# Two edits at the attention's joint: the norm weights' loads are queued behind the output units' loads, and the second tokens' queries are computed in two halves of the features

## The chip, the cores and the metric

One core of a Trainium2 chip runs the whole kernel. The metric is device time in microseconds (us). Three runs of the kernel before gave a median of 1199.4 us (1196.8 to 1199.63). One more execution was taken with the hardware profiler: it took 1191.01 us, with a span of 1189.2 us from the first to the last recorded instruction. All durations below come from that one execution.

## The reference, cut to what matters

The network has two layers of width 1024 over 256 tokens. Around the change each layer does this (l is the layer, `ng` its eight norm weights):

```
h = mixer(...)                                  # layer 0: RWKV and retention, layer 1: sparse attention and short convolution
x = x + rms_norm(concat(y_a, y_b) @ w_out, ng[3])
q = (rms_norm(x, ng[4]) @ wq)                   # 256 tokens x 512 features, 4 heads of 128
s = q . k * 128**-0.5 ; prob = softmax(s)       # k and v of 256 memory tokens, computed earlier
x = x + rms_norm((prob . v) @ wo, ng[5])
x = x + 0.5 * rms_norm(swiglu(rms_norm(x, ng[6])), ng[7])
```

So at the joint of mixer and attention two norms follow each other: weight `ng[3]` on the mixer's output, and, after the sum into x, weight `ng[4]` ahead of the query projection.

## The kernel before

The 256 tokens are two tiles of 128 tokens, called t = 0 and t = 1. Every weight is taken in units of 128 x 1024 numbers. A unit is loaded by a DMA of SyncE's queue (SP) into a staging tile `wst`, rounded by ScalarE (ACT) into a high part `whi` ("hi"), and VectorE (DVE) subtracts that from the unit to get the low part `wlo` ("lo"). A product is then three matmuls (high by high, low by high, high by low) that add up in one PSUM bank. A PSUM bank holds 512 float32 numbers in each of 128 partitions, and one call of `bank` takes one whole bank.

`cross` is the function of the change, and it runs once in each layer. It first takes four output units of the mixer (`w_out`, the "head"), each with its load, hi and lo. The other four output units (the "tail") open a list `units_ahead`, followed by the four units of `wq`, the four of `wo` and those of the next FFN. `ahead.load(n)` issues the next n loads; later each `lo` issues one load more. Of every five loads of the list the first three go to a ring of three staging tiles, the fourth and fifth to a ring of two in the pool "norm". The norm weights (`gain`, tile `gb`, 128 x 1024, one row copied to all partitions, ring of three in that same pool) are loaded on SP's queue too, and the call of `tc.issue_after` puts each behind the load that was written last before it. For the rest, what is not fixed in this way on SP stands in the order of the framework's planner.

From `bridge` on, the order of TensorE (PE), DVE and ACT is the order in which the code is written (`in_order`). The part that the second edit touches runs as follows for each layer. PE turns the last normalized tokens (`trh`), and projects the first half of the sums for the queries of t = 1 (`project` with the wq units 0 and 1: 12 matmuls of 512 columns into the bank `pq[1]`). Then it computes the scores of t = 0 (`scores`, tile `psc`), and with units 2 and 3 the second half of the sums for the queries of t = 1 (12 more matmuls into the same bank). Meanwhile DVE works on the lo's, finds each row's maximum (`highest`), and ACT takes the exponentials of t = 0 (`exps`, four instructions and their sums). Behind those stands `query(1)` on ACT, a copy of the bank (tile `qn`), on which PE's transposes `trq` (`query_t(1)`) wait.

In `project`, matmuls for unit j are written as 4 matmuls with the high part of the tokens (line 429), and 2 with the low part, one unit later (line 434). The retention code of layer 0 has four small products into one bank, each copied out by ACT before the next one is written (lines 1271 and 1272). They are not changed, but the prediction reads them.

Of the kernel before, what the change touches and what calls it, by code (L numbers as in the profile page):

```python
# [10 lines left out]
F32 = mybir.dt.float32  # L11
F32R = mybir.dt.float32r
AF = mybir.ActivationFunctionType
# [4 lines left out]
P = 128  # L18
# [76 lines left out]
def tile_hybrid_trunk(ctx: ExitStack, tc: tile.TileContext, a: dict, out: bass.AP, stop=None):  # L95
    nc = tc.nc
# [12 lines left out]
    def bank(tag, name):  # L109
        return psum.tile([P, 512], F32, name=name, tag=tag)  # L110
# [7 lines left out]
    def new_h(p, shift=48):  # L118

        return tuple(p.tile([P, DT * S + 64], F32R, name=name, bufs=1)[:, shift:shift + DT * S].rearrange(  # L120
            "p (k n) -> p k n", k=DT) for name in ("hhi", "hlo"))
# [80 lines left out]
    def wload(w, k0, kt, c0, n):  # L202
        src = w[k0 * P:(k0 + kt) * P, c0:c0 + n].rearrange("(k p) n -> p k n", p=P)
        def load(t):
            env["loaded"] = nc.sync.dma_start(t, src).ins

        return [load], kt, n
# [4 lines left out]
    def nat(w, n=512):  # L212
        return [wload(w, 2 * i, 2, 0, n) for i in range(4)]

    class units_ahead:
# [22 lines left out]
        def hi(self):  # L238
            st, kt, n, *only = self.staged.pop(0)
            hi, lo, v = unit_tiles(kt, n, *only)  # L240
            nc.scalar.activation(hi[:, :kt * n], st[:, :kt * n], AF.Copy)  # L241
            self.open.append((st, hi, lo, kt * n))
            self.units.append((v(hi), v(lo)))

        def lo(self):
            st, hi, lo, m = self.open.pop(0)
            env["split"] = nc.vector.tensor_sub(lo[:, :m], st[:, :m], f32(hi[:, :m])).ins  # L247
            self.load()
# [57 lines left out]
    def gain(ap, offset):  # L306
        g = env["norm"].tile([P, D], F32, name="gb", bufs=3)
        if "loaded" in env:
            with behind(env["loaded"]):
                row(g, ap, offset, D, eng=nc.sync)  # L310
        else:
            row(g, ap, offset, D)
        return g
# [99 lines left out]
    ng = lambda l, i: gain(a["norm_g"], (l * 8 + i) * D)  # L413
# [4 lines left out]
    def in_order():  # L418
        return tc.manual_schedule(engines={ET.DVE, ET.Activation, ET.PE})

    def project(ps, h, t, us, js):

        s = slice(t * P, (t + 1) * P)
        for j in (*js, None):
            if j is not None:
                for i in range(2):
                    k = 2 * j + i
                    for n in range(2):
                        nc.tensor.matmul(ps, h[0][:, k, s], us[j][n][:, i, :], start=k == 0 and n == 0, stop=False)  # L429
            if j != js[0]:  # L430
                p = js[-1] if j is None else js[js.index(j) - 1]
                for i in range(2):
                    k = 2 * p + i
                    nc.tensor.matmul(ps, h[1][:, k, s], us[p][0][:, i, :], start=False, stop=k == DT - 1)
# [188 lines left out]
    def cross(l, sp, y, w_unit, w_out, kts):  # L623
# [4 lines left out]
        h, h2 = new_h(sp), new_h(sp)  # L628
        cx = ExitStack()
        xp = cx.enter_context(tc.tile_pool(reuse_waits="tile", name=f"xa{l}", bufs=1))  # L630
        gp, gn = ng(l, 3), ng(l, 4)
        head = len(kts) - 4

        def products(pss, t, q, y, us, first, last, ks, js):
            s, c = slice(t * P, (t + 1) * P), slice(q * 512, (q + 1) * 512)
            for j in js:
                k, u = ks[j], us[j]
                mm3(pss[t][q], (y[0][:, k, s], y[1][:, k, s]), (u[0][:, 0, c], u[1][:, 0, c]), first and j == 0,
                    last and j == len(ks) - 1)

        pss = [[bank(tag, "po") for tag in ("iv", "bk")] for _ in range(2)]
        for i in range(head):
            u = w_unit(kts[i])
            for t in range(2):
                for q in range(2):
                    products(pss, t, q, y, [u], i == 0, False, [kts[i]], (0,))
        tail = kts[head:]
        ahead = units_ahead([(*wload(w_out, k, 1, 0, D), wpool) for k in tail] + nat(wq) +
                            [wload(wo, k, 1, 0, D) for k in range(4)] + nat(wg) + nat(wu), env["norm"])
        ahead.load(5)  # L650
        kT = xp.tile([P, 4, S], F32, name="kT")
        vM = xp.tile([P, 2, 512], F32, name="vM")
        wsrc["i"] = 0
# [11 lines left out]
        o = new_h(keep, 0)  # L665
        pq, qn, qT, pr, mx, sm, pT, sps, nb = [{} for _ in range(9)]

        def query(t):
            qn[t] = xp.tile([P, 512], F32, name="qn", bufs=2)
            nc.scalar.activation(qn[t], pq[t], AF.Copy)  # L670

        def query_t(t):
            tr = bank("pa", "trq")
# [53 lines left out]
        def warm():  # L727
            nc.scalar.activation(small.tile([P, 1], F32, name="warm", tag="rstd"), ones, AF.Exp)

        with in_order():  # L730
            V = nc.vector
            hi, lo, units = ahead.hi, ahead.lo, ahead.units
            po = [post(pss[t], gp, t, False) for t in range(2)]
            no = [rms(env["x"][:, t, :], gn, h, t) for t in range(2)]
            tp = lambda t, q: products(pss, t, q, y, us, head == 0, True, tail, range(4))
            bridge(tp, po, no, ahead, 2 + l * 0)
            pq[0] = bank("pa", "pq")
            project(pq[0], h, 0, units, (0, 1, 2))
            po[1].root()
            po[1].gain(1)  # L740
            gn2 = ng(l, 6)
            warm()
            hi()
            po[1].add(0)
            po[1].add(1)
            no[1].square(0)
            no[1].gain(0)
            no[1].square(1)
            no[1].root()
            no[1].gain(1)  # L750
            project(pq[0], h, 0, units, (3,))
            query(0)
            no[1].scale(0, V)
            no[1].scale(1)
            no[1].turn(0)
            query_t(0)
            no[1].turn(1)
            lo()
            hi()
            lo()  # L760
            pq[1] = bank("pa", "pq")
            project(pq[1], h, 1, units, (0, 1))
            hi()
            lo()
            scores(0, 0)
            highest(0, 0)
            scores(0, 1)
            highest(0, 1)
            exps(0, 0)
            exps(0, 1)  # L770
            project(pq[1], h, 1, units, (2, 3))
            soft(0)
            query(1)
            hi()
            lo()
            query_t(1)
            soft_t(0)
            scores(1, 0)
            highest(1, 0)
            hi()  # L780
            lo()
            exps(1, 0)
            values(0)
            scores(1, 1)
            highest(1, 1)
            exps(1, 1)
            hi()

            pss = [[bank(tag, "po") for tag in ("iv", "bk")] for _ in range(2)]
            tp = lambda t, q, js=range(4): products(pss, t, q, o, units[4:8], True, True, range(4), js)  # L790
            po = [post(pss[t], gp2, t, False) for t in range(2)]
            no = [rms(env["x"][:, t, :], gn2, h2, t) for t in range(2)]
            tp(0, 0)
            soft(1)
            lo()
            hi()
            po[0].square(0)
            po[0].gain(0)
            lo()
            tp(0, 1, (0, 1))  # L800
            soft_t(1)
            hi()
            lo()
            tp(0, 1, (2, 3))
            po[0].square(1)
            po[0].root()
            values(1, 0, 2)
            po[0].gain(1)
            values(1, 2, 4)
            po[0].add(0)  # L810
            po[0].add(1)
            no[0].square(0)
            no[0].gain(0)
            no[0].square(1)
            no[0].root()
            no[0].gain(1)
            hi()
            tp(1, 0)
            no[0].scale(0, V)
            no[0].scale(1)  # L820
            lo()
            tp(1, 1, (0, 1, 2))
            no[0].turn(0)
            no[0].turn(1)
            po[1].square(0)
            po[1].gain(0)
            tp(1, 1, (3,))
            po[1].square(1)
            po[1].root()
            po[1].gain(1)  # L830
            hi()
            lo()
            pg = bank("pa", "pg")
            project(pg, h2, 0, units[8:12], range(4))
            po[1].add(0)
            po[1].add(1)
            hi()
            no[1].square(0)
            no[1].gain(0)
            no[1].square(1)  # L840
            no[1].root()
            no[1].gain(1)
            lo()
            no[1].scale(0, V)
            no[1].scale(1)
            hi()
            lo()
            pu = bank("pa", "pu")
            project(pu, h2, 0, units[12:16], (0, 1))
            no[1].turn(0)  # L850
            no[1].turn(1)
            project(pu, h2, 0, units[12:16], (2, 3))
# [767 lines left out]
    with stage("0", None, None, 4) as sp:  # L1620
        env["x"] = sp.tile([P, 2, D], F32, name="x", bufs=1)
        h = new_h(sp)
# [70 lines left out]
```

## Time and profile before

| what | value |
|---|---|
| median of 3 runs | 1199.4 us (1196.8 to 1199.63) |
| the profiled execution, span | 1191.01 us, 1189.2 us |
| PE busy, of the span | 96% |
| DVE busy | 61% |
| ACT busy | 51% |
| DMA, mean | 180 GB/s |
| granted PE clock, mean | 0.994 |

Busy shares are means over stages with different limits. PE's 96% says that almost any stall of PE adds to the span, and that few such stalls are left. `cross` fills about 404 to 485 us in layer 0 and 933 to 1008 us in layer 1, and shows several of them. In a timeline each row has its start, its length, the engine, the line, output <- inputs, the tile and the count; in square brackets stands how long the engine was idle before it, and what it waited for. PEld is PE's loading of the stationary operand, which runs beside the matmuls. The rows of matmuls overlap, so that their pace is read from their starts.

### The profile page before, as it was taken

To read this page: it belongs to the slowest core of one execution; us is meant where nothing else is said; L and a number is where in the kernel's file an instruction comes from. 1 tells how busy PE (TensorE), PEld (TensorE's weight loads), DVE (VectorE), ACT (ScalarE), POOL (GpSimd) and SP (SyncE) were. 2 spreads that over 40 slices of the span, in tenths; PEclk is the share of its full clock that TensorE was granted. 3 is DMA by queue.
4 is the path that set the end of the run, shared out by engine and by line. 5 is a ranking of instruction groups with operands and counts; after the bars stand their busy time and mean duration, and the time that the engine had idled before them with its cause. 6 is when DMAs were issued, how large, how long until landed. Compare 5 with 4: busy or idle time off the path is not lost.

```text
span 1189.2 us, 19763 instructions
## 1 busy us (share of the span) xinstructions
PE 1144.7 (96%) x7956; PEld 1011.5 (85%) x7956; DVE 728.5 (61%) x1097; ACT 606.8 (51%) x908; POOL 69.2 (6%) x104
## 2 busy tenths in 40 slices
PE   6999999999998999999999999999999999999997
PEld 4899999987776777899999799999788778899996
DVE  5546656587666678655554756544679577655552
ACT  5545555754334467554443645443556566554441
POOL 0000000011341000000000000000100000000000
PEclk9999999999999999999999999999999999999999
DMA  6777764644552765477665377665423753676650
GB/s 218 229 265 230 219 208 159 204 138 126 156 158 89 212 247 163 134 238 214 192 190 165 108 252 226 197 198 150 141 89 93 254 204 106 214 226 198 194 161 36
DMA packets 152267, 213.99 MB, mean 180 GB/s; under 512 B 21872, under 2 KB 115184, under 8 KB 152176
## 3 DMA queue, kind: packets, MB, share of 16 engines
q1 hardware_dynamic: 138224, 206.58, 56.0%
q10 hardware_dynamic: 13216, 3.54, 1.3%
q0 software_dynamic: 736, 2.62, 0.6%
q8 instruction: 62, 1.02, 0.3%
q14 instruction: 29, 0.24, 0.1%
HBM read 206.67 MB, written 6.05 MB: 179 GB/s over the span
## 4 chain that ended last, share of the span: by engine, by line
PE 78%; DVE 10%; ACT 4%; DMA 3%; issue 3%; POOL 2%; SPq 0%; ACTq 0%; POOLq 0%; DVEq 0%
PE pd L257 6%; PE pd L256 6%; PE pd L258 6%; PE pg L256 6%; PE pu L256 6%; PE pg L257 6%; PE pg L258 6%; PE pu L258 6%; PE pu L257 6%; PE pu L429 1%; PE trh L353 1%; DVE wlo L247 1%; DVE wlo L199 1%; PE pg L429 1%; POOL rstd L304 1%
## 5 line engine op out<-in xcount | busy, mean ns | idle before, releaser
L199 DVE TENSOR_TENSOR wlo<-wst,whi 128x1024 fp32r<-128x1024 f32 x290 | 355.2, 1229 | 291.3 <-ACT whi L198 289.8
L198 ACT ACTIVATE whi<-wst 128x1024 fp32r<-128x1024 f32 x290 | 306.0, 1060 | 314.8 <-PE pg L257 57.9
L256 PE MATMUL pu<-hhi,whi 128*128 128x256 f32 x576 | 160.8, 279 | 0.0
L256 PE MATMUL pg<-hhi,whi 128*128 128x256 f32 x576 | 160.7, 279 | 0.0
L258 PE MATMUL pu<-hhi,wlo 128*128 128x256 f32 x576 | 160.5, 279 | 0.0
L257 PE MATMUL pu<-hlo,whi 128*128 128x256 f32 x576 | 160.5, 279 | 0.0
L257 PE MATMUL pg<-hlo,whi 128*128 128x256 f32 x576 | 160.5, 279 | 0.0
L258 PE MATMUL pg<-hhi,wlo 128*128 128x256 f32 x576 | 160.4, 279 | 0.0
L257 PE MATMUL pd<-wlo,ahi 128*128 128x512 f32 x352 | 138.1, 393 | 0.0
L256 PE MATMUL pd<-whi,ahi 128*128 128x512 f32 x352 | 137.7, 392 | 0.0
L258 PE MATMUL pd<-whi,alo 128*128 128x512 f32 x352 | 137.7, 392 | 0.0
L256 PEld LDWEIGHTS pg<-hhi,whi 128*128 128x128 f32 x576 | 108.2, 188 | 1.4
L257 PEld LDWEIGHTS pg<-hlo,whi 128*128 128x128 f32 x576 | 108.2, 188 | 1.4
L258 PEld LDWEIGHTS pu<-hhi,wlo 128*128 128x128 f32 x576 | 109.3, 190 | 0.0
L258 PEld LDWEIGHTS pg<-hhi,wlo 128*128 128x128 f32 x576 | 109.2, 190 | 0.0
L256 PEld LDWEIGHTS pu<-hhi,whi 128*128 128x128 f32 x576 | 108.2, 188 | 0.0
L257 PEld LDWEIGHTS pu<-hlo,whi 128*128 128x128 f32 x576 | 108.1, 188 | 0.0
L247 DVE TENSOR_TENSOR wlo<-wst,whi 128x1024 fp32r<-128x1024 f32 (+1 forms) x68 | 81.8, 1215 | 42.0 <-ACT whi L241 41.2
L241 ACT ACTIVATE whi<-wst 128x1024 fp32r<-128x1024 f32 (+1 forms) x68 | 70.3, 1053 | 37.8 <-PE pu L257 9.3
L304 POOL TENSOR_TENSOR rstd<-s,hneg 128x1 f32<-128x1 f32 x34 | 23.9, 703 | 942.4 <-DVE s L374 942.4
L258 PEld LDWEIGHTS pd<-whi,alo 128*128 128x128 f32 x352 | 66.1, 188 | 14.8 <-DVE alo L252 0.6
L256 PEld LDWEIGHTS pd<-whi,ahi 128*128 128x128 f32 x352 | 66.1, 188 | 14.1 <-ACT ahi L251 0.7
(374 smaller groups left out, 2010.4 us busy)
## 6 DMA issues: line engine op xcount, KB each, us to landing
wst<-in_ffn_w_gate_dram SPq DMA_DIRECT2D x88, 512.0 KB, 4.6
wst<-in_ffn_w_up_dram SPq DMA_DIRECT2D x88, 512.0 KB, 4.4
wst<-in_ffn_w_down_dram SPq DMA_DIRECT2D x88, 512.0 KB, 4.3
wst<-in_ev_w_in_dram SPq DMA_DIRECT2D x30, 512.0 KB, 4.1
gb<-in_norm_g_dram SPq DMA_DIRECT2D x16, 512.0 KB, 6.0
wst<-in_od_w_in_dram SPq DMA_DIRECT2D x12, 512.0 KB, 4.3
wst<-in_xa_wk_dram SPq DMA_DIRECT2D x8, 512.0 KB, 4.2
wst<-in_xa_wv_dram SPq DMA_DIRECT2D x8, 512.0 KB, 4.2
```

The costliest lines, as they stand in the source:

```text
L198: nc.scalar.activation(hi[:, :m], st[:, :m], AF.Copy)
L199: env["split"] = nc.vector.tensor_sub(lo[:, :m], st[:, :m], f32(hi[:, :m])).ins
L241: nc.scalar.activation(hi[:, :kt * n], st[:, :kt * n], AF.Copy)
L247: env["split"] = nc.vector.tensor_sub(lo[:, :m], st[:, :m], f32(hi[:, :m])).ins
L256: nc.tensor.matmul(ps, l_hi, r_hi, start=first, stop=False)
L257: nc.tensor.matmul(ps, l_hi, r_lo, start=False, stop=False)
L258: nc.tensor.matmul(ps, l_lo, r_hi, start=False, stop=last)
L304: nc.gpsimd.tensor_tensor(dst, src, hneg[:, :n], op=ALU.pow)
L353: nc.tensor.transpose(tr[:, i * P:(i + 1) * P], self.xg[q][:, i * P:(i + 1) * P], ident)
L429: nc.tensor.matmul(ps, h[0][:, k, s], us[j][n][:, i, :], start=k == 0 and n == 0, stop=False)
```

## The change

The loads of `gp` (weight `ng[3]`) and `gn` (weight `ng[4]`) were the first statement of `cross`, ahead of the head units. Now `gp` is written behind the fourth load of the list (the last tail unit), and `gn` behind the fifth (the first unit of `wq`).

The queries of t = 1 were summed over units 0 and 1 for all 512 features, and later over units 2 and 3. Now `query_half(0)` sums over all four units for features 0 to 255, `query_half(1)` later for features 256 to 511, in the other half of the same bank. Each is 24 matmuls of 256 columns in place of 12 of 512. The copy `query(1)` becomes two of 128 x 256. The first stands behind `exps(0, 1)` on ACT and ahead of `query_half(1)` in the code, the second where the whole copy stood.

```diff
-        gp, gn = ng(l, 3), ng(l, 4)
...
-        ahead.load(5)
+
+        ahead.load(4)
+        gp = ng(l, 3)
+        ahead.load(1)
+        gn = ng(l, 4)
...
-        def query(t):
-            qn[t] = xp.tile([P, 512], F32, name="qn", bufs=2)
-            nc.scalar.activation(qn[t], pq[t], AF.Copy)
+        def query(t, q=None):
+            if not q:
+                qn[t] = xp.tile([P, 512], F32, name="qn", bufs=2)
+            c = slice(0, 512) if q is None else slice(q * 256, (q + 1) * 256)
+            nc.scalar.activation(qn[t][:, c], pq[t][:, c], AF.Copy)
...
             pq[1] = bank("pa", "pq")
-            project(pq[1], h, 1, units, (0, 1))
+
+            columns = lambda q: slice(q * 256, (q + 1) * 256)
+            query_half = lambda q: project(pq[1][:, columns(q)], h, 1,
+                                           [tuple(z[:, :, columns(q)] for z in u) for u in units], range(4))
+            query_half(0)
             hi()
             lo()
             scores(0, 0)
...
             exps(0, 0)
             exps(0, 1)
-            project(pq[1], h, 1, units, (2, 3))
+            query(1, 0)
+            query_half(1)
             soft(0)
-            query(1)
+            query(1, 1)
             hi()
             lo()
             query_t(1)
```

## Rows read from the trace of the kernel before

**Rows 1.** The page: busy time by engine, and the norm weights' loads.
```profile
PE 1144.7 (96%) x7956; PEld 1011.5 (85%) x7956; DVE 728.5 (61%) x1097; ACT 606.8 (51%) x908; POOL 69.2 (6%) x104
...
gb<-in_norm_g_dram SPq DMA_DIRECT2D x16, 512.0 KB, 6.0
```

**Rows 2.** Timeline of layer 0, around the second half of the queries.
```profile
448.03 1.89 PE L686 MATMUL psc<-kT,qT 128*128 128x256 f32 x8
...
449.56 0.58 PE L429 MATMUL pq<-whi,hhi 128*128 128x512 f32 x1
...
451.11 0.48 ACT L701 ACTIVATE pr<-psc,nb 128x256 f32<-128x256 f32 x1 [3.13 <-DVE nb L695]
...
451.60 1.08 PE L434 MATMUL pq<-whi,hlo 128*128 128x512 f32 x4
...
452.92 0.61 ACT L670 ACTIVATE qn<-pq 128x512 f32<-128x512 f32 x1
...
453.58 0.66 PE L675 MATMUL trq<-ident,qn 128*128 128x128 f32 x4 [0.90 <-ACT qn L670]
```

**Rows 3.** Timeline of layer 1, the same place.
```profile
975.39 0.65 PE L675 MATMUL trq<-ident,qn 128*128 128x128 f32 x4 [0.91 <-ACT qn L670]
```

**Rows 4.** Timeline of PE in an FFN: first and last of 24 matmuls of 256 columns.
```profile
143.37 0.28 PE L256 MATMUL pg<-hhi,whi 128*128 128x256 f32 x1
...
146.00 0.28 PE L258 MATMUL pg<-hhi,wlo 128*128 128x256 f32 x1
```

**Rows 5.** Timeline of ACT: a copy of 128 x 256 out of PSUM.
```profile
988.38 0.39 ACT L251 ACTIVATE hhi<-pot 128x256 fp32r<-128x256 f32 x1
```

**Rows 6.** Timeline of layer 0's retention: four products in one bank, each copied out.
```profile
407.56 0.28 ACT L1272 ACTIVATE kv<-pkv 128x128 f32<-128x128 f32 x1 [1.35 <-PE pkv L1271]
...
407.88 0.30 PEld L1271 LDWEIGHTS pkv<-vr,ra 128*128 128x128 f32 x2 [0.33 <-ACT kv L1272]
```

**Rows 7.** Two stalls of PE; windows (busy by engine, PEclk, DMA share, GB/s); matmuls after.
```profile
369.80 0.44 PE L1174 MATMUL pyt<-ident,yn 128*128 128x128 f32 x2 [3.39 <-DVE yn L1171]
...
372.08 0.63 PE L258 MATMUL prq<-whi,hlo 128*128 128x512 f32 x1
372.51 0.63 PE L256 MATMUL prq<-whi,hhi 128*128 128x512 f32 x1
...
435.07 1.92 PE L353 MATMUL trh<-ident,xn 128*128 128x128 f32 x8 [2.01 <-DVE xn L346]
...
432.00:436.00 4.00, 1.99 (x10) 1.52 (x9) 3.21 (x6) 2.52 (x7) 0.94 (x1) 0.89 0.95 384
436.00:440.00 4.00, 4.00 (x15) 3.19 (x14) 3.19 (x7) 3.80 (x7) 0.55 (x1) 0.69 0.83 319
```

**Rows 8.** Timelines of layer 1: SP, ACT, PE and DVE around the last output unit.
```profile
936.41 0.90 SPq L137 DMA_DIRECT2D gb<-in_norm_g_dram  x2
937.35 1.00 SPq L205 DMA_DIRECT2D wst<-in_od_w_out_dram  x1
...
945.52 2.25 ACT L241 ACTIVATE whi<-wst 128x1024 fp32r<-128x1024 f32 x2 [2.87 <-DMA wst<-in_od_w_out_dram]
...
945.88 0.39 PE L258 MATMUL po<-whi,hlo 128*128 128x512 f32 x1
...
947.89 0.50 PE L257 MATMUL po<-wlo,hhi 128*128 128x512 f32 x1 [0.76 <-DVE wlo L247]
...
947.97 1.06 ACT L241 ACTIVATE whi<-wst 128x1024 fp32r<-128x1024 f32 x1 [0.20 <-DMA wst<-in_xa_wq_dram]
...
952.22 0.22 DVE L374 TENSOR_SCALAR s<-ssp 128x1 f32<-128x1 f32 x1 [0.20 <-ACT sq L391]
```

**Rows 9.** Timelines of layer 0: SP, ACT and DVE around the last output units.
```profile
407.98 0.81 SPq L205 DMA_DIRECT2D wst<-in_ev_w_out_dram  x2
...
417.11 3.91 ACT L241 ACTIVATE whi<-wst 128x1024 fp32r<-128x1024 f32 x4 [2.43 <-PE po L258]
...
426.29 0.68 DVE L398 TENSOR_TENSOR u<-po,gb 128x512 f32<-128x512 f32 x1
```

## The prediction

> **What bounds the kernel now.** I read the page first. PE is busy for 96% of the span [rows 1]. DVE and ACT, at 61% and 51%, have room on the whole. So work that leaves DVE or ACT gains nothing by itself, and a stall of PE costs its full length. The second view was the timeline of the joint in both layers, with the question what PE waits for there and how long; the third was SP's own rows, for the moved loads. The reader is to see two stalls that the change could touch. PE waits 0.90 us in layer 0 and 0.91 us in layer 1 for the copy of the second tokens' queries [rows 2, 3], and in layer 1 it runs into the late last output unit [rows 8].
>
> **The split queries.** The matmul work is the same. In an FFN 24 matmuls of 256 columns start from 143.37 to 146.00: 23 steps, 0.114 us each, and the last one's 0.28 us ends 2.91 us after the first start [rows 4]. The 12 of 512 columns at the joint run from 449.56 to 451.60 + 1.08 = 452.68, 3.12 us, in which the restart behind the scores is contained [rows 2]. I take 3.0 us for one half of the features after a restart. Twice as many matmuls therefore cost nothing on PE. On ACT, a 128 x 256 copy out of PSUM took 0.39 us [rows 5] where the whole copy took 0.61 [rows 2]; two halves are 0.78, 0.17 more.
>
> The split's cost lies elsewhere: both halves are in one PSUM bank, and the first half's copy is written ahead of the second half's matmuls. What such an order does is shown by the retention code, which writes four products into different columns of one bank and has ACT copy each out. The copy at 407.56 ends at 407.84; PE's next load for the next columns starts at 407.88, after 0.33 us of waiting, and its releaser is that copy, though the product needs nothing that the copy makes [rows 6]. So a matmul into other columns of the bank waits for the reader of the first ones. Before, all writes into `pq[1]` came ahead of its one reader, and this wait could not arise.
>
> The page "PSUM — Partial Sum Buffer" of the Trainium skill, section "PSUM bank collisions raise a hardware error", has a rule that speaks against the edit: accesses by two engines are to be guarded by bank and not by address, since disjoint columns of one bank collide as well. By that rule the sum has the wait worked out next in both layers; if addresses alone were guarded it would be rival C's. The trace agrees with the rule, with the 0.33 us of rows 6.
>
> Now the place of the new wait. The half copy stands on ACT behind the four exponentials of the first tokens. They can't start before 451.11, since DVE, with its three lo's ahead of the maxima, has the bias ready only then (ACT idles 3.13 us), and ACT is through with them at 452.92, when the whole copy starts [rows 2]. Nothing ahead of this changes. So the half copy runs from 452.92 to 453.31, and `query_half(1)` starts at about 453.36 (0.05 from a copy's end to PE's restart, as from 453.53 to 453.58). Before, that work started at 449.56, underneath the exponentials. Behind the waiting matmul everything is queued: on PE `query_t(1)`, the turns of the probabilities, the second scores; on ACT `query(1, 1)`, and behind it the next hi, on which DVE's next lo and with it SP's next load depend. The written order lets none of it pass, so all moves by the same amount, and no later wait is shortened.
>
> The sum for layer 0: start 453.36, + 3.0 of matmuls, + 0.04 to ACT, + 0.39 second half copy, + 0.05 = 456.84 for `trq`, against 453.58. That is +3.27 us. The 0.22 us that the smaller copy saves is in it. Layer 1 has the same pattern (`trq` at 975.39 after 0.91 us [rows 3]; its whole copy began at the same distance ahead of it), so +3.27 again. Bounds: 0.17 each if no wait arises (below), 3.5 if the half copy costs as much as the whole.
>
> **The clock.** In the new stall PE has nothing from the end of the scores, 448.03 + 1.89 = 449.92 [rows 2], to 453.36: 3.4 us in each layer. The trace has stalls of 3.39 and 2.01 us, and after both the matmuls run at half pace: after the longer, starts are 0.43 us apart at 512 columns [rows 7], where twice the 0.114 of rows 4 is 0.23. Around the shorter, the granted clock is 0.89 and 0.69 over two stretches of 4 us; with only two levels, 2.4 and 1.2 GHz, that is (0.11 + 0.31) x 4 / 0.5 = 3.4 us at 1.2 GHz [rows 7]. In these 3.4 us PE does 0.23/0.43 = 53% of its work, which loses 1.6 us. The new stalls are as long as the longer one, so I add 1.6 us in each layer. Bounds: 0 (no fall), and 3.2 (a second such stretch, or one whose effect spreads).
>
> **The moved loads.** In layer 1 the two norm loads are issued at 936.41, ahead of the last output unit at 937.35, whose hi starts at 945.52 after 2.87 us of waiting for that DMA; PE's step from 945.88 to 947.89 takes 2.0 us where two steps of 0.23 would do, a loss of 1.55 us [rows 8]. With the new order this load goes first, about 0.9 us earlier and with two transfers less ahead of it, so that wait goes. What is late next is the second `wq` unit. Its hi, at 947.97, waits for its DMA as well (0.20) [rows 8], and ahead of this load stand the same transfers as before, only in another order. Through this hi and the lo's behind it, DVE reaches the sum of squares at 952.22 after a mere 0.20 us of idleness [rows 8], and on it hangs the chain of the norms that ends this part of the joint. So of 1.55 us I let 0.2 pass through and have PE wait for the rest a little later. Bounds: -1.55 (all passes), and +0.5 if SP, whose queue is moved too, gets a norm load that blocks a unit behind it. The norm weights themselves are covered: such a load lands 6.0 us after issue in the median [rows 1], and issued at some 937 to 939 they are first read when the products of the last output unit, at 947.89, are under way [rows 8].
>
> In layer 0 the last two output units are issued at 407.98 to 408.8, their hi's start at 417.11 behind PE (2.43 us of waiting for PE, none for a DMA), and `gp` is first read at 426.29, 17 us after it can now be issued [rows 9]. The edit is worth 0 there; without that cover it would cost at most the landing time of one load.
>
> **Sum.** 2 x 3.27 + 2 x 1.6 - 0.2 = +9.5 us. Against the profiled execution's own 1191.0 us that makes 1200.5. That execution was 8.4 us faster than the median of the runs shown; stalls and steps of this kind don't depend on that, so I put the difference on the median: 1199.4 + 9.5 = 1208.9, rounded to 1209.
>
> **The rivals.**
> A. The bank wait arises, but the clock holds in one layer or in both: +6.3 to +7.9, 1205.7 to 1207.3. For it speaks that a fall need not begin right after each stall; against it, that both stalls of 2 us and more in rows 7 have one.
> B. The wait arises and more is lost: two stretches of half clock in a layer, or the moved loads hold SP's queue: +11 to +14, 1210 to 1213. For it: the slow stretch falls on PE's chain of projection, turns and scores, on which ACT and DVE wait in their turn. Against: neither row shows more than the one stretch.
> C. The halves do not wait for each other, so not slower than before. Place: the first matmul of `query_half(1)`. Price: ACT is busy until 452.92 all the same, then copies two halves, so `trq` comes at 453.75, +0.17 per layer; with the loads' -0.2 to -1.55 the total is -1.2 to +0.1, 1198.2 to 1199.5. It decides from the point where PE's matmuls for features 256 to 511 start ahead of the first half copy. For it: the columns are disjoint. Against it: rows 6.
> D. As C, and the joint's later waits shrink with it, for over 3.6 us. I find no row from which that much could come: the two `trq` waits are 1.8 us together [rows 2, 3], the late unit 1.55.
>
> **How the numbers follow.** Forecast 0.52 (1208 to 1210.5), A 0.22, B 0.11, C 0.12, D 0.03. What can be told from no change is about 0.3%, 3.6 us. The forecast, A and B lie above that: slower 0.84, taking a little off for the spread of the median. C is "same", with that little: 0.13. D is "faster": 0.03. The range 1202 to 1214 holds the forecast, A and B with some 2.5 us for the spread of the runs on either side, and leaves out C and D. The likeliest case's own range is 1206 to 1212.
>
> **What would show it.** Right: the first matmul of 256 columns for `pq[1]`'s second half waits more than 3 us for ACT's `qn`; that `qn` of 128 x 256 follows the exponentials directly; `trq` comes some 3 us later against the scores; the granted clock drops to half in the 4 us after it, in both layers. In layer 1 the last output unit's hi no longer waits for its DMA, and the second `wq` unit's still does. Wrong: `query_half(1)` directly behind the scores (C); a stall without a drop of the clock (A); or a sum of squares in layer 1 that comes over 1 us earlier relative to the head's end, which would give the loads' edit its full 1.55 us.

## The result: 0.81% slower, and the profile after

The changed kernel took 1205.9 us in the median of 7 runs, the kernel before 1196.8 in 7 runs beside it. The ratio is 1.0081, with an interval of 1.0063 to 1.0100: +9.7 us, 7.5 to 12. The forecast was +9.5, put on a median of 1199.4 from three runs: 1208.9. With a median before of 1196.8, the measured 1205.9 lies 3 us below that. The two profiled executions, 1206.0 and 1191.0 us, lie further apart than that, by 15.0 us, and where these 15 us are is the first thing to read.

The page after has the shares of busy time of before [rows 1] to within a point; nothing about the change can be read from it:

```profile
PE 1151.6 (96%) x8004; PEld 1019.2 (85%) x8004; DVE 728.2 (60%) x1097; ACT 607.4 (50%) x910; POOL 69.0 (6%) x104
```

The timeline of layer 0 around the second half of the queries answers to [rows 2]:

```profile
449.70 1.89 PE L691 MATMUL psc<-kT,qT 128*128 128x256 f32 x8
...
452.82 0.47 ACT L706 ACTIVATE pr<-psc,nb 128x256 f32<-128x256 f32 x1 [3.13 <-DVE nb L700]
...
454.63 0.39 ACT L675 ACTIVATE qn<-pq 128x256 f32<-128x256 f32 x1
455.07 0.29 PEld L429 LDWEIGHTS pq<-whi,hhi 128*128 128x128 f32 x1 [3.88 <-ACT qn L675]
455.07 0.58 PE L429 MATMUL pq<-whi,hhi 128*128 128x256 f32 x1 [3.48 <-ACT qn L675]
...
459.50 1.06 PE L434 MATMUL pq<-whi,hlo 128*128 128x256 f32 x4
...
460.36 1.11 PE L680 MATMUL trq<-ident,qn 128*128 128x128 f32 x4
460.60 0.38 ACT L675 ACTIVATE qn<-pq 128x256 f32<-128x256 f32 x1 [5.58 <-PE pq L434]
```

The half copy `qn` stands behind the exponentials, and PE's first matmul of the second half waits 3.48 us for it, as forecast. What wasn't forecast is the length of what follows: the 24 matmuls run from 455.07 to 460.56, 5.49 us, where the forecast had 3.0 at full clock and 1.6 more for the fall of the clock. Layer 1 answers to [rows 3] with the same pattern:

```profile
984.43 0.58 PE L429 MATMUL pq<-whi,hhi 128*128 128x256 f32 x1 [3.39 <-ACT qn L675]
...
989.72 0.51 PE L680 MATMUL trq<-ident,qn 128*128 128x128 f32 x2
989.96 0.38 ACT L675 ACTIVATE qn<-pq 128x256 f32<-128x256 f32 x1 [5.58 <-PE pq L434]
```

Windows of 4 us over both places, as in [rows 7]; the granted clock is the third number from the end:

```profile
452.00:456.00 4.00, 0.93 (x4) 0.93 (x5) 2.63 (x9) 2.20 (x9) 0.00 (x0) 0.76 0.88 326
456.00:460.00 4.00, 4.00 (x21) 4.00 (x20) 0.13 (x1) 0.00 (x0) 0.00 (x0) 0.50 0.02 7
460.00:464.00 4.00, 3.83 (x25) 3.09 (x25) 1.59 (x2) 3.40 (x6) 0.00 (x0) 0.89 0.00 0
...
980.00:984.00 4.00, 1.04 (x5) 0.57 (x3) 2.81 (x6) 1.82 (x9) 0.00 (x0) 0.89 0.94 297
984.00:988.00 4.00, 3.56 (x16) 3.57 (x17) 1.32 (x5) 0.38 (x3) 0.00 (x0) 0.50 0.25 96
988.00:992.00 4.00, 3.71 (x23) 3.20 (x22) 0.68 (x1) 2.04 (x4) 0.00 (x0) 0.75 0.00 0
```

A granted clock of 0.76 over 4 us means 0.24 x 4 / 0.5 = 1.9 us at 1.2 GHz. With 4.0 and 0.9 us in the next two windows that is 6.8 us in layer 0, and 6.9 in layer 1 by the same sum: twice the 3.4 us of [rows 7].

Around layer 1's last output unit, SP, ACT and PE answer to [rows 8]:

```profile
944.70 0.42 SPq L137 DMA_DIRECT2D gb<-in_norm_g_dram  x1
945.17 0.43 SPq L205 DMA_DIRECT2D wst<-in_xa_wq_dram  x1
945.64 1.11 SPq L137 DMA_DIRECT2D gb<-in_norm_g_dram  x1
...
953.87 2.00 ACT L241 ACTIVATE whi<-wst 128x1024 fp32r<-128x1024 f32 x2 [3.35 <-DMA wst<-in_xa_wq_dram]
...
955.93 0.50 PE L256 MATMUL po<-whi,hhi 128*128 128x512 f32 x1 [1.80 <-ACT whi L241]
...
957.19 0.49 PE L257 MATMUL po<-wlo,hhi 128*128 128x512 f32 x1 [0.76 <-DVE wlo L247]
```

In the kernel before, PE's row between the two of [rows 8] was this:

```profile
946.63 0.49 PE L256 MATMUL po<-whi,hhi 128*128 128x512 f32 x1 [0.37 <-ACT whi L241]
```

Before, the row of two hi's waited for the `w_out` load, and PE went on at 946.63, right behind the first of them. Here it waits for a `wq` load, and PE goes on only at 955.93, behind the second. So the first hi of the pair is now that of the first `wq` unit, and the output unit's stands behind it: the order in which ACT takes them has changed, though the diff doesn't touch it. The output unit's hi is written ahead of the part with the fixed order (`in_order`), the `wq` unit's in it, so that the order of the two is left to the planner, and it placed them the other way about. A `wq` load now goes out between the norm loads; that this is its reason is not shown.

So the 15.0 us, measured along PE's chain between rows of the same operation: 1.9 had arisen before layer 0's first changed step (the first `por` at 403.30 and 405.21), 5.8 and 5.7 lie in the two joints, 1.4 at the last output unit of layer 1, and +0.2 in what is left. The 1.9 are spread between executions: a second profile of the changed kernel (e11) has its first `por` at 401.98. So the ratio is the better measure of the whole.

### The profile page after: what moved, and what is told of

Same layout as the page of the kernel before. It is cut to its first block, busy times and chain, and to the rows that moved or that the text cites. A ratio compares the mean times of both kernels' runs of the same rounds, so it can differ in the third digit from the quotient of the medians.

```text
span 1204.2 us, 19858 instructions
## 1 busy us (share of the span) xinstructions
PE 1151.6 (96%) x8004; PEld 1019.2 (85%) x8004; DVE 728.2 (60%) x1097; ACT 607.4 (50%) x910; POOL 69.0 (6%) x104
## 4 chain that ended last, share of the span: by engine, by line
PE 69%; DVE 12%; DMA 7%; ACT 5%; issue 3%; POOL 2%; SPq 0%; ACTq 0%; DVEq 0%; POOLq 0%
PE pu L256 6%; PE pd L257 6%; PE pd L256 6%; PE pu L257 5%; PE pu L258 5%; PE pd L258 5%; PE pg L256 5%; PE pg L257 5%; PE pg L258 5%; DVE wlo L199 2%; ACT whi L198 1%; PE pu L429 1%; DVE wlo L247 1%; PE trh L353 1%; DMA wst<-in_xa_wq_dram 1%
```

## The experiments

Two stretches are compared in all of them. The **joint** runs from the first tokens' scores (first `psc`) to the first product with the values (first `pot`): before, 448.03 to 455.98 in layer 0 and 969.83 to 977.79 in layer 1. The **head** ends in layer 0 at that `psc` and begins at the retention's first `por`; in layer 1 it runs from ACT's hi of the fourth-last output unit (936.15) to the turn of h (`trh`, 957.34). "Fall" is the time at half clock from the stall on, worked out from windows as above. The heads hold falls of the clock of their own, which this column leaves out; they come up with e6 to e8.

| kernel | joint, layer 0 / 1 | fall, layer 0 / 1 | head, layer 0 / 1 | ratio to before (95%) |
|---|---|---|---|---|
| before | 7.95 / 7.96 | 0 / 0 | 44.73 / 21.19 | 1 |
| after | 13.73 / 13.65 | 6.8 / 6.9 | 44.49 / 22.59 | 1.0081 (1.0063–1.0100) |
| e1 loads only | 7.94 / 7.95 | 0 / 0 | 45.15 / 22.40 | 1.0020 (1.0008–1.0031) |
| e2 split only | 12.78 / 11.25 | 3.4 / 0 | 43.40 / 22.09 | 1.0075 (1.0052–1.0099) |
| e3 copy early | 7.86 / 7.87 | 0 / 0 | 44.63 / 22.83 | 1.0003 (0.9987–1.0019) |
| e4 two banks | 7.95 / 7.97 | 0 / 0 | 44.93 / 22.74 | 1.0013 (0.9997–1.0029) |
| e5 warm stall | 11.36 / 11.25 | 0 / 0 | 45.26 / 22.13 | 1.0046 (1.0028–1.0064) |
| e6 edge on ACT | 12.79 / 13.64 | 3.4 / 6.9 | 43.87 / 20.71 | 1.0066 (1.0044–1.0089) |
| e7 early and edge | 7.86 / 7.87 | 0 / 0 | 43.33 / 21.61 | 0.9990 (0.9969–1.0011) |
| e8 loads and edge | 7.94 / 7.95 | 0 / 0 | 44.67 / 21.55 | 0.9991 (0.9979–1.0003) |
| e9 late copy | 7.95 / 7.96 | 0 / 0 | 44.56 / 21.91 | 0.9996 (0.9976–1.0017) |
| e10 split only | 12.62 / 12.62 | 3.4 / 3.4 | 45.09 / 22.03 | one execution |
| e11 after | 13.64 / 12.59 | 6.8 / 3.4 | 44.83 / 24.91 | one execution |
| e12 split only | 12.46 / 11.26 | 3.4 / 0 | 43.36 / 23.31 | one execution |

**The loads alone (e1)**

```
-        gp, gn = ng(l, 3), ng(l, 4)
...
-        ahead.load(5)
+        ahead.load(4)
+        gp = ng(l, 3)
+        ahead.load(1)
+        gn = ng(l, 4)
```

> The kernel before with the moved loads alone; the queries stay whole. Theory (T): the loads' edit costs 1.0 to 1.6 us, all of it in layer 1, because in the changed kernel ACT has the hi of the first wq unit ahead of the hi of the last output unit and so waits there for wq's load. Expected: ratio to the kernel before 1.001, within 0.3%; in layer 1 the last output unit's hi starts behind a hi that waits for a wq load, and the turn of h (trh) comes about 1.4 us later after the head's work than before. At the joint PE's wait for the copy of the second queries stays at about 0.9 us. Rival (R1), the prediction: the late unit's wait goes and 0.2 us is gained, trh 0.2 us earlier. Rival (R2): the loads carry much of the whole loss (over 4 us), since what they delay meets the split: then this kernel is 0.3% or more slower than before by itself.

The ratio, 1.0020, is small and on the slow side: +2.4 us, 1.0 to 3.7. The joints are those of before to 0.01 us. ACT has the order of the changed kernel:

```profile
951.81 2.00 ACT L241 ACTIVATE whi<-wst 128x1024 fp32r<-128x1024 f32 x2 [3.21 <-DMA wst<-in_xa_wq_dram]
...
953.87 0.50 PE L256 MATMUL po<-whi,hhi 128*128 128x512 f32 x1 [1.65 <-ACT whi L241]
```

So the prediction's -0.2 us (R1) is refuted by this run, and the loads don't carry much of the loss by themselves (R2, 0.3% or more, is met only by the upper end of the interval).

**The split alone (e2)**: the changed kernel with the moved loads of e1 taken back.

> The changed kernel with the norm loads back at their old place: only the split of the queries is left. Theory (T): the wait of some 3.4 us for the half copy and the half-clock stretch stand in both layers, 5.5 to 5.8 us each, so 11 to 12 us more than the kernel before in the traces, and at least 1.006 as a ratio; in layer 1 the last output unit's hi stands on ACT where it stood before. Rival (R1): split and loads need each other (the loads' delay brings about the long half-clock stretch): then the stall stays at 3.4 us, but the matmuls behind it take about 4.3 us instead of 5.5, and the sum is 7 to 9 us.

The ratio carries nearly the whole loss, 1.0075. The stall is there in both layers, 3.39 and 3.40 us. The clock, though, behaved differently in the two layers of this one execution:

```profile
452.00:456.00 4.00, 4.00 (x24) 4.00 (x23) 0.57 (x3) 0.00 (x0) 0.00 (x0) 0.57 0.02 7
...
980.00:984.00 4.00, 0.77 (x6) 0.77 (x7) 2.63 (x10) 2.21 (x9) 0.00 (x0) 1.00 0.92 329
984.00:988.00 4.00, 3.75 (x32) 3.38 (x30) 0.56 (x3) 1.64 (x3) 0.00 (x0) 1.00 0.03 12
```

In layer 1 it holds at 1.00, and there the joint shows the wait by itself: 11.25 - 7.96 = 3.29 us, beside the 3.27 of the prediction. Layer 0 has 1.53 more for its 3.4 us at half clock. My expectation of 11 to 12 us over both was too high, as it took the long fall of the first profile for the rule; the two joints add 8.1 us. That is the sum that R1 gave, and its reason, that the loads bring about the long fall, needed e10 to e12.

**The half copy ahead of the exponentials (e3)**

```
+            query(1, 0)
             exps(0, 0)
             exps(0, 1)
-            query(1, 0)
             query_half(1)
```

> The changed kernel with one line moved: the copy of the first half of the second queries is written ahead of the exponentials of the first tokens, where ACT idled 3.13 us. Both halves stay in one PSUM bank. Theory (T): what costs is the place of the half copy on ACT behind the exponentials. Then the matmuls of the second half start straight behind the scores, within 0.3 us, the granted clock doesn't fall there, and the turn of the second queries comes 0.2 us earlier after the scores than in the kernel before (a copy of 0.39 us instead of 0.61 is last). Ratio to before 1.000 to 1.002 (the loads' part of 1.4 us is still in it), so 0.6% or more below the changed kernel. Rival (R1): the split itself costs, by twice as many matmuls of half the size: then 2 us or more per layer remain over the kernel before, with no wait in front of them. Rival (R2): the half copy ahead of the exponentials delays these by 0.4 us and all behind them by as much.

```profile
448.01 0.38 ACT L675 ACTIVATE qn<-pq 128x256 f32<-128x256 f32 x1 [0.31 <-PE pq L434]
449.35 0.47 PE L429 MATMUL pq<-whi,hhi 128*128 128x256 f32 x1
...
452.37 0.38 PE L680 MATMUL trq<-ident,qn 128*128 128x128 f32 x2
...
452.64 0.39 ACT L675 ACTIVATE qn<-pq 128x256 f32<-128x256 f32 x1
...
453.09 0.44 PE L680 MATMUL trq<-ident,qn 128*128 128x128 f32 x2 [0.34 <-ACT qn L675]
```

The copy fits into ACT's idle 3 us, the second half starts behind the scores with no wait, and the joint is 0.09 us shorter than before. Twice as many matmuls of half the size cost nothing that can be seen; both rivals fall. The last two turns of the queries start 5.28 us behind the first scores, where the row of turns started at 5.55 before: 0.27 us earlier, about the 0.2 that I expected. Of that 0.09 us are left at the end of the joint, and this is the gain of the split where nothing stands in its way.

**Two banks (e4)**: the written order stays, and the second half gets a bank of its own.

```
...
             query(1, 0)
+            pq[1][1] = bank("pa", "pq")
             query_half(1)
```

> The changed kernel with the two halves of the second queries in two PSUM banks, written order unchanged: the half copy stays behind the exponentials. Theory (T): the wait arises because both halves share one bank. Then the matmuls of the second half no longer wait for the half copy, the clock doesn't fall, and the turn of the second queries comes 0.2 us later after the scores than in the kernel before (two copies of 0.39 us instead of one of 0.61). Ratio to before 1.000 to 1.003. Rival (R1): the matmuls wait for the copy for another reason than the shared bank (the queries' tile, the order written): then the stall of 3.4 us and the ratio of about 1.008 stay. Rival (R2): the second bank is not free in time, as other products hold it: then a shorter wait, with another releaser than the half copy, takes its place.

```profile
450.60 0.47 PE L429 MATMUL pq<-whi,hhi 128*128 128x256 f32 x1
...
453.89 0.67 ACT L675 ACTIVATE qn<-pq 128x256 f32<-128x256 f32 x2
454.34 0.71 PE L680 MATMUL trq<-ident,qn 128*128 128x128 f32 x4 [0.56 <-ACT qn L675]
```

No stall and no fall, with the half copy exactly where it stood in the changed kernel. So it is the shared bank that makes the matmuls wait, and rivals R1 and R2 are out. One thing stays mixed: each call of `bank` gives one tile for one bank, so the second half got a tile of its own too, and whether the wait goes by the tile or by the bank this run can't tell. A tile in itself need not be waited for as a whole: in e3 the first two turns read `qn` at 452.37, ahead of the second half copy into that tile at 452.64. Two copies at the end, 0.67 us for the pair instead of 0.61, leave the joint at 7.95 and 7.97; the turns don't come later, though I had expected 0.2 us. In the program the wait is one of PE on ACT's copy; whether the chip would do without it wasn't tried.

**PE kept busy in the stall (e5)**

```
             query(1, 0)
+            fill = bank("fr", "fill")
+            for i in range(14):
+                nc.tensor.matmul(fill, h[0][:, i % 8, P:2 * P], units[i % 4][0][:, 0, :], start=True, stop=True)
             query_half(1)
```

> The changed kernel with 14 more matmuls of 512 columns, whose output nobody reads, between the scores and the second half of the second queries: PE works in the stall instead of standing still (14 x 0.227 us is 3.2 us of the 3.4). Theory (T): the bank wait of 3.29 us and the half-clock stretch are two losses, and the second is brought about by PE's standing still. Then the half copy's place and the wait for it stay, the granted clock behind it is 1.00, the 24 matmuls take 3.0 us instead of 5.5, and from the first scores to the first product with the values it is 11.2 to 11.3 us in both layers, as in layer 1 of the kernel without the moved loads, where the clock happened to hold (11.25). That is 2.4 us a layer below the changed kernel's profile: ratio to before 1.005 to 1.008. Rival (R1): the slow matmuls behind the stall come from their size or from the restart: then they take 5.5 us also here, and the ratio is 1.008 or more.

```profile
980.61 3.57 PE L783 MATMUL fill<-whi,hhi 128*128 128x512 f32 x14
984.35 0.39 PE L429 MATMUL pq<-whi,hhi 128*128 128x256 f32 x1 [0.17 <-ACT qn L675]
...
980.00:984.00 4.00, 4.00 (x19) 3.14 (x17) 2.72 (x6) 1.91 (x9) 0.00 (x0) 1.00 0.95 298
984.00:988.00 4.00, 3.57 (x28) 3.16 (x28) 1.32 (x5) 0.81 (x4) 0.00 (x0) 1.00 0.25 96
```

The wait for the copy stands, useful work starts no earlier, and the clock stays at 1.00 in both layers; layer 1's joint is 11.25 us, the value of e2 where the clock happened to hold. This doesn't rest on the one profile: the mean granted clock of the 12 executions is 0.9934, as in e1 (0.9935), where the changed kernel has 0.9894 over 8. More work on PE made the kernel faster, 1.0046 against 1.0081, a little more than I expected (1.005 to 1.008). So the loss has two parts, and the second comes of PE's standing still.

**The order on ACT (e6, e7, e8)**: an edge keeps the hi of the early `wq` units behind the last output unit's.

```
-            nc.scalar.activation(hi[:, :kt * n], st[:, :kt * n], AF.Copy)
+            env["whi"] = nc.scalar.activation(hi[:, :kt * n], st[:, :kt * n], AF.Copy).ins
...
-        with behind(env["split"]):
+        with behind(env["split"]), behind(env["whi"]):
```

> The changed kernel with an order edge on ACT: the hi of the first wq units stay behind the hi of the attention's last output unit, as they did in the kernel before. The queries stay split. Theory (T): of what the moved loads cost in layer 1, 1.2 to 1.6 us, all comes from the hi of the first wq unit that stands ahead of the last output unit's hi on ACT and waits for its load. Then the output unit's hi starts with no wait for a wq load, and from the hi of the first output unit seen on ACT to the turn of h it is 21.0 us, against 21.19 before and 22.59 in the changed kernel; the stall at the queries is as in the changed kernel. Ratio to before 1.0065. Rival (R1): the unit is late through its DMA, which the norm loads hold up: then it is 22 us or more, with ACT waiting for the w_out load.

> The changed kernel with both cures: the half copy ahead of the exponentials, and the hi of the wq units behind the last output unit's. Theory (T): 0.09 us a layer is gained at the queries against the kernel before, and 0 to 0.2 us at the norms in layer 1, where the prediction put the moved loads' worth; in all -0.2 to -0.5 us, ratio 0.999 to 1.001, which can't be told from no change. Rival (R1): the moved loads free the whole wait of the last output unit (1.55 us) once ACT's order is as before: then -1.7 us, ratio 0.998 to 0.999.

> The kernel before with the moved loads and with the order edge that keeps the hi of the first wq units behind the last output unit's; the queries stay whole. The traces so far have, from the retention's first por to the first scores in layer 0, 44.1 us with the loads at the old place (2 traces), 44.9 with them moved (5) and 43.6 with moved loads and the edge (2); and from the first output unit's hi to the turn of h in layer 1, 21.6, 22.5 and 21.2. Theory (T): the loads' cost is ACT's order alone, so with the edge the two stretches are at 43.3 to 43.9 and 20.7 to 21.6, and the ratio to before is 0.998 to 1.000, where the moved loads without the edge gave 1.002. Rival (R1): the transfers' order itself costs: then the ratio stays at 1.0015 to 1.0025.

ACT's row at the same place, first in e6, then in e8:

```profile
949.84 2.01 ACT L241 ACTIVATE whi<-wst 128x1024 fp32r<-128x1024 f32 x2 [1.61 <-PE po L258]
```

```profile
945.35 1.06 ACT L241 ACTIVATE whi<-wst 128x1024 fp32r<-128x1024 f32 x1 [1.61 <-PE po L258]
947.18 1.06 ACT L241 ACTIVATE whi<-wst 128x1024 fp32r<-128x1024 f32 x1 [0.78 <-DMA wst<-in_xa_wq_dram]
949.72 1.06 ACT L241 ACTIVATE whi<-wst 128x1024 fp32r<-128x1024 f32 x1 [1.47 <-DMA wst<-in_xa_wq_dram]
```

The output unit's hi waits for PE alone, as in layer 0 before [rows 9], and PE's wait for it is gone. Over all profiles that wait is 0.37, 1.31, 1.25 and 0.94 us with the loads at the old place (before, e2, e10, e12), 1.12 to 2.54, in the mean 1.78, with them moved (7 profiles), and nothing with the edge (3). The means of the heads are 44.1 / 22.2 us at the old place, 44.8 / 22.8 moved, 44.0 / 21.3 with the edge, but most of that in layer 0 is the clock. The heads of layer 0 are of two kinds, as these windows over the whole head show, the first in the kernel before, the second in e2:

```profile
403.30:448.03 44.73, 40.56 (x193) 31.78 (x192) 35.10 (x68) 26.82 (x47) 5.83 (x6) 0.96 0.66 236
```

```profile
402.83:446.23 43.40, 38.99 (x204) 31.06 (x203) 35.13 (x68) 27.05 (x47) 5.83 (x6) 1.00 0.68 242
```

Ten heads have a clock of 0.96, by the fall of [rows 7] at the turn of h, and take 44.5 to 45.3 us. Four (e2, e6, e7, e12) have 1.00 and take 43.3 to 43.9. Among the ten the means are 44.9 at the old place, 44.8 moved, 44.7 with the edge: the order on ACT makes no difference there that can be seen. All 7 heads with moved loads have the fall, 2 of 4 at the old place and 1 of 3 with the edge; that the loads bring it about is not shown. In e8 the layer 0 head, 44.67, lies outside of what I expected for this reason, and the ratio inside.

In layer 1 the heads of e11 and e12 hold a fall too; without these two the means are 21.8, 22.4 and 21.3. With the edge, what is late next is the `wq` unit: in e8 two `wq` hi's wait 0.78 and 1.47 us for their loads, as the prediction had it. And PE's wait is not saved, it moves on to the turn of h, as the prediction had it too; the first row is from before, the second from e8:

```profile
957.34 1.09 PE L353 MATMUL trh<-ident,xn 128*128 128x128 f32 x8 [0.50 <-DVE xn L346]
```

```profile
958.79 1.60 PE L353 MATMUL trh<-ident,xn 128*128 128x128 f32 x8 [2.13 <-DVE xn L346]
```

That wait is 1.28, 2.18 and 2.13 us in e6, e7 and e8, and in e7 and e8 the clock falls behind it, which the head no longer covers: from the turn of h to the scores it is 13.2 and 13.0 us there, elsewhere 12.5. From the first hi of the head to the scores, layer 1 takes 34.3 us in the mean at the old place, 35.0 moved and 34.2 with the edge (33.3, 34.8 and 34.5), e11 and e12 left out. e7, the version that the experiments point to, and e8 are at 0.9990 and 0.9991; both intervals reach over 1, so neither can be told from the kernel before. The ratio leaves R1 of e7, a gain of 1.7 us, undecided; its own profile speaks against it, with 34.8 us for this stretch and PE's wait moved on.

**The half copy behind the matmuls (e9)**

```
-            query(1, 0)
             query_half(1)
+            query(1, 0)
```

> The changed kernel with two lines changed about: the copy of the first half of the second queries is written behind the matmuls of the second half, in the same bank. Theory (T): it is the order in which reader and writer of the one bank are written that makes the matmuls wait. Then they start straight behind the scores, there is no fall of the clock, and from the first scores to the first product with the values it is 7.9 to 8.0 us in both layers, as with two banks (7.95, 7.97). Ratio to before 1.001 to 1.002, which is the loads' part. Rival (R1): with both half copies last, the second one waits for the first and all moves by 0.4 us a layer: 8.3 us.

```profile
450.63 0.47 PE L429 MATMUL pq<-whi,hhi 128*128 128x256 f32 x1
...
453.93 0.67 ACT L675 ACTIVATE qn<-pq 128x256 f32<-128x256 f32 x2
```

One bank, and no wait: the joint is that of e4. Two lines changed about give back the whole of the split's cost. The 8.3 us of R1 are not seen, as the two copies follow each other in 0.67 us. The ratio, 0.9996, is a little under what I expected, with 1.001 to 1.0017 inside its interval.

**How long the fall is (e10, e11, e12)**: e2, the changed kernel and e2 again, unedited.

> The kernel with the split queries alone, profiled once more: how long is the half-clock stretch behind the stall, when nothing in the program has changed? So far it was 3.4 us in layer 0 and none in layer 1 with the loads at the old place, 6.8 and 6.9 us in the changed kernel, 3.4 and 6.9 us with the order edge. Theory (T): the stretch varies from execution to execution and from layer to layer, whatever the loads do; so another pair of lengths is seen here, out of none, 3.4 and 6.9 us, and the joint takes 11.25, 12.8 or 13.7 us accordingly. Rival (R1): it hangs on the loads' place; then again 3.4 us and none.

> The changed kernel, profiled once more. Theory (T): the half-clock stretches are drawn anew out of none, 3.4 and 6.9 us, and at least one of the two joints differs from the first profile's 13.7 us. Rival (R1): with the moved loads they are 6.8 and 6.9 us again.

> The kernel with the split queries alone, a third profile, for the same question. Theory (T): again a pair out of none, 3.4 and 6.9 us; over all profiles that have the stall and no filler, the mean cost of the fall is 1.2 to 2.2 us a layer. Rival (R1): 3.4 us and none.

Layer 1 of the changed kernel in its second profile:

```profile
984.00:988.00 4.00, 0.76 (x3) 0.76 (x4) 2.63 (x10) 2.21 (x9) 0.00 (x0) 0.85 0.92 329
988.00:992.00 4.00, 3.89 (x25) 3.66 (x23) 0.30 (x2) 0.29 (x2) 0.00 (x0) 0.72 0.03 13
```

That is 3.4 us at half clock, where the first profile had 6.9. e10 has 3.4 in both layers, e12 has 3.4 and none, as e2. So one program, behind the same stall of 3.4 us, loses 0 to 1.5 us (e2, e10, e12), and the changed kernel 1.3 to 2.5 us. Over the 12 joints that have the stall and no filler, the fall costs 1.5 us in the mean (the joint less 11.25).

That the lengths are drawn anew is borne out; that they are so "whatever the loads do" is not. With the loads moved 4 of 6 falls were long, at the old place none of 6, and the granted clocks of all executions, profiled or not, point the same way. Their mean is 0.9894 over 8 executions of the changed kernel, where kernels with moved loads and no stall have 0.9938 (e1, e3, e4, e9); it is 0.9924 over 8 of the split alone, where the kernel before has 0.9944 over 81. Since 0.001 of some 1200 us is 2.4 us at half clock, that makes about 5 us a joint with the loads moved and 2.5 us at the old place. The executions were on several chips, and no run shows how the loads would do it. The cause stays open.

## Why the prediction was right, and where it was wrong

- **The wait for the bank: right.** +3.27 us a layer was forecast (its terms as written add up to 3.26); where the clock holds it is +3.29 (e2, layer 1) and +3.29 (e5, layer 1). e4 and e9 show both of its conditions: take away the shared bank, or the order in which it is written, and it is gone. Only a small term was off: the 0.17 us that two copies were to cost, 2 x 0.39 against 0.61, is 0.06 as measured (0.67 for the pair), and 0.00 in the joint. Rival C needed the matmuls to start ahead of the half copy, and they did so only in e3, e4 and e9.
- **The clock: right in kind, a mean for the size.** 1.6 us a layer was taken, with 0 and 3.2 as bounds. The 12 joints have 0 to 2.5 and a mean of 1.5, but this is a mean over three kernels: 2.2 in the changed kernel's four joints, 2.0 in e6's two, 0.9 in the six of the split alone. In the changed kernel's first profile both layers had the long fall, 2.4 to 2.5 us, which the text counted under rival B; its second has one long and one short. The Trainium skill, page "TensorE: Matmul & The Clock Gate", section "Part 1: The HAM clock gate (the "warmup" mystery)", says that the number of slow matmuls at the start of the same kernel varies from run to run. Here it varies behind a stall as well, from none to all 24.
- **The moved loads: wrong, the step that failed.** "So of 1.55 us I let 0.2 pass through" reckoned with the transfers' order and left ACT's as it was. The planner that stands between the written order and ACT placed the first `wq` unit's hi ahead of the output unit's, and the edit cost where it should have gained. The sign that "the last output unit's hi no longer waits for its DMA" came true to the letter, but the hi waited behind another one's DMA. PE's wait there went from 0.97 us in the mean to 1.78, and layer 1's way to the scores grew by 0.7 us (35.0 against 34.3). In the time of the whole kernel the size is less sure: four kernels with the moved loads and no stall (e1, e3, e4, e9) lie 0.8 thousandths above before in the mean, 1.0 us, and only e1's interval excludes none. So the term was a cost of some 0.7 to 1.0 us instead of -0.2. With ACT's order mended the rest of the step holds: the second `wq` unit is late next (e8), PE waits at the turn of h instead (2.18 and 2.13 us in e7 and e8, 0.50 before), and 0.1 us passes through (34.2 against 34.3), which is less than the spread of the profiles. Layer 0, counted at 0, shows no cost beside the draws of the clock.
- **The sum.** 2 x 3.29 + 2 x 1.5 + 1.0 = 10.6 us by the steps as measured, +9.7 (7.5 to 12) by the ratio, +9.5 forecast. The largest term was right for its reason. That the whole came out within 0.2 us is in part luck: the changed kernel's own joints lose 2.2 us to the clock where 1.6 was taken, the loads' term had the wrong sign, and the interval is 4.5 us wide.

## What to carry to other kernels

A product can be split so that its first part is copied out early. If both parts share a PSUM bank and the copy is written between them, the second part waits for that copy, wherever it stands in its engine's queue. The whole gain here was 0.09 us a layer, and the wait cost 3.29. Put the copy where its engine is idle, or behind the second part, or give the parts two banks. When a load is moved, look at the order that a planner gives to the work fed by it, not only at the transfers. Count a stall of PE with the half-clock stretch behind it, as a mean, since one profile shows only one draw.

## What had not been expected of the hardware

The fall of the clock came in three sizes behind stalls that differ by no more than 0.1 us: none, 3.4 us (3.36 to 3.44) and 6.8 to 6.9 us. It began at different points too: inside the stall in the changed kernel (1.9 us of the window that ends at 456 are at half clock, the matmuls start at 455.07), and in e2's layer 0 only when the matmuls had run for a microsecond at 0.12 us each. Shorter waits came with a fall too: of PE's waits for the turn of h in layer 0, ten of 1.6 to 2.8 us did, and four of 1.1 to 1.7 us did not. And 14 matmuls that nobody needs, put into each stall, took about 0.35% off the time (1.0046 against 1.0081; the two intervals just touch).
